# A split-precision decoder trunk on one core: the order of the wide and the narrow products at the end of a column tile

## The chip, the cores and the metric

The kernel runs on one core of a Trainium2 chip. The metric is the device time of one execution in microseconds (us); less is better. Three executions were timed for the kernel before, and one more was taken with the hardware profiler, which is where every row below comes from.

## What is computed

Two layers, each with a SwiGLU feed-forward block, a mixing block and a second SwiGLU block; after each of them a residual is added and a LayerNorm applied. There are 256 tokens of 1024 channels, the feed-forward width is 2816, everything is float32. The change lies in the first two products of the feed-forward block:

```python
def swiglu(x, w_gate, w_up, w_down):
    return (jax.nn.silu(x @ w_gate) * (x @ w_up)) @ w_down

for l in range(DEPTH):
    f = swiglu(x, ffn_w_gate[l, 0], ffn_w_up[l, 0], ffn_w_down[l, 0])
    x = layer_norm(ALPHA * x + 0.5 * f, ln_g[l, 0], ln_b[l, 0])
    z = x @ w_in[l]
    y = ...  # three mixers on column groups of z
    x = layer_norm(ALPHA * x + y @ w_out[l], ln_g[l, 1], ln_b[l, 1])
    f = swiglu(x, ffn_w_gate[l, 1], ffn_w_up[l, 1], ffn_w_down[l, 1])
    x = layer_norm(ALPHA * x + 0.5 * f, ln_g[l, 2], ln_b[l, 2])
```

## The kernel before

**Split operands.** Each float32 operand is held as two float32r halves, a high one and a low one (`split`: ScalarE copies the high half, VectorE subtracts it from the source to get the low half). A product of two split operands is high x high + high x low + low x high, summed in PSUM. The weights `wh` and `wl` are such halves of blocks of 128 x 1024 that arrive by DMA in `raw`; `xT` holds both halves of the transposed activations.

**Column tiles.** Gate and up columns are taken 128 at a time ("T" units; 44 tiles of this kind in the first feed-forward block, 38 in each of the other three). One tile uses one weight block, one of 12 in a ring, and one PSUM bank of 8. The inner dimension of 1024 is walked in eight steps k = 0 to 7 (`KD` is 8). In a step the weights are the stationary operand and the tokens are the moving one:

- the **wide** product, `wh` times `xTb[k]`: 512 columns, since `xTb` shows the high and the low half of the 256 tokens side by side. It fills the whole bank: high x high in the first 256 columns, high x low in the last 256.
- the **narrow** product, `wl` times `xT[k, 0]`: 256 columns, added to the first half of the bank.

`sub_T` calls the step eight times for one tile; then `total` adds the two halves of the bank: ScalarE copies `b[S:]` to `hh`, VectorE adds `b[:S]`. Four tiles (two gate, two up) make a unit, with a Tanh, a multiply and a `split` of the result into `hTh`, `hTl` behind them. In the first feed-forward block `first_unit` computes the first four tiles together instead: there the inner loop goes over four banks, and the outer one over k. The first columns of the other three blocks are done in another form (tokens stationary), and the down projection too; both use products of 512 columns throughout. The mixer's column tiles use `mm_T`, three products of 256 columns in a step.

**Order.** TensorE runs in the order of the program. For ScalarE, VectorE and the DMA queue a list scheduler (`Program.issue`) sets the order from costs and due times; its cost of a product is (columns + 16)/2.4 ns. It writes the order when the program is built; the chip then follows it.

In the step, before the change, the wide product stands first for k = 0 to 6 and last for k = 7. So a tile runs wide, narrow, ... wide, narrow, narrow, wide, and the next tile begins with a wide one.

Of the kernel before, what the change touches and what calls it, by code (L numbers as in the profile page):

```python
# [18 lines left out]
S = 256  # L19
L = 2  # L20
DFF = 2816
KD = D // P
# [256 lines left out]
def build(tc, a):  # L279
# [7 lines left out]
    def ap(v, dtype=None):  # L287
        return v.ap(dtype) if isinstance(v, View) else v
# [35 lines left out]
    def walk(x):  # L324
        return x.rearrange("p (a b c) -> p b a c", b=RUNS, c=RUN)

    def mm(out, lhsT, rhs, start, stop, cost=None, runs=None, both=False):

        cost = cost or (out.n + 16) / 2.4

        def go():
            o, x = ap(out), ap(rhs)
            if runs is not None:
                x = walk(x)[:, runs]
                o = walk(o) if both else o
            T.matmul(out=o, lhsT=ap(lhsT), rhs=x, start=start, stop=stop)  # L336
        pr.add("T", cost, [lhsT, rhs], [out], go)
# [13 lines left out]
    def buf(name, shape, dtype=F32, pool=None, **kw):  # L351
        b = Buf(name, shape, dtype, phase=opened.get(pool), **kw)
        (cbufs if pool is None else phases[pool]).append(b)
        return b
# [21 lines left out]
    xT = buf("xT", (KD, 2, S), F32R, off=OFF_X)  # L376
    xTb = xT.alias((KD, 2 * S))
# [19 lines left out]
    def bank(*shape):  # L397
        b = bank_fifo.pop(0)
        return b.alias(shape) if shape else b
# [27 lines left out]
    ALL = slice(0, RUNS)  # L427
# [12 lines left out]
    def mm_TT(b, h, l, k):  # L440


        def joined(stop):
            mm(b.all, h, xTb[k, :], k == 0, stop, runs=ALL, both=True)

        if k < KD - 1:
            joined(False)
        mm(b[:S], l, xT[k, 0, :], False, False, runs=ALL, both=True)
        if k == KD - 1:
            joined(True)  # L450

    def total(out, b):

# [108 lines left out]
    def ffn(layer, i, ln_prev, nxt, mid=None):  # L562
# [35 lines left out]
        for j, (kind, c0, n) in enumerate(units):  # L598
            if kind == "nat":
                continue  # L600
            f, m = c0 // P, n // P
            if kind == "first":
                first_unit(take(4), th, hh, hTh, hTl)
                continue
            b = take(2 * m)
            for q in range(m):
                pg = bank()
                sub_T(pg, b[q], mm_TT)
                total(hh[q, :], pg)
            act(th[:m, :], hh[:m, :], AF.Tanh, scale=0.5)  # L610
            stt(th[:m, :], th[:m, :], 1.0, hh[:m, :], ALU.add, ALU.mult)
            for _ in range(2):
                if todo:
                    hT(*todo.pop(0))
            for q in range(m):
                pu = bank()
                sub_T(pu, b[m + q], mm_TT)
                total(hh[q, :], pu)
            tt(hh[:m, :], th[:m, :], hh[:m, :], ALU.mult)
            split(hTh[f:f + m, :], hTl[f:f + m, :], hh[:m, :])  # L620
            if mid and j == 3:
                mid()
        return down(hTh, hTl, NF, TAIL, 4.0 * ALPHA, 16.0 * EPS, last, nxt)

    def first_unit(b, th, hh, hTh, hTl):

        accs = [bank() for _ in range(4)]
        for k in range(KD):
            i = b[k // 2] % RING
            for j in range(4):  # L630
                cs = slice((k % 2) * 512 + j * P, (k % 2) * 512 + (j + 1) * P)
                mm_TT(accs[j], wh[i][cs], wl[i][cs], k)
        for j in range(2):
            total(hh[j, :], accs[j])
            act(th[j, :], hh[j, :], AF.Tanh, scale=0.5)
            stt(th[j, :], th[j, :], 1.0, hh[j, :], ALU.add, ALU.mult)
            total(hh[j, :], accs[2 + j])
            tt(hh[j, :], th[j, :], hh[j, :], ALU.mult)
            split(hTh[j, :], hTl[j, :], hh[j, :])
# [224 lines left out]
    b = bank()  # L864
# [127 lines left out]
```

## Time and profile before

| | |
|---|---|
| time, median of 3 (lowest to highest) | 892.92 us (892.76 to 893.49) |
| the profiled execution's own time | 893.46 us |
| its span, first to last instruction | 891.4 us, so 2.06 us lie around it |
| granted TensorE clock, mean | 0.998 of full |
| TensorE (PE), weight loads (PEld) | busy 882.3 us (99%), 781.0 us (88%) |
| VectorE (DVE), ScalarE (ACT) | busy 654.7 us (73%), 483.9 us (54%) |
| DMA queue of the weights | 57.3% of 16 engines' time |

A row of the trace gives the time at which a product starts, and a modelled duration that reaches beyond the start of the next product, since products are pipelined. What a product costs is therefore read from start to start.

### The profile page before, as it was taken

The numbers are of one execution on the slowest core, as the hardware profiler recorded it, in microseconds if no ns is written. First come the engines' busy times: TensorE is split into PE (matmuls) and PEld (weight loads), VectorE is DVE, ScalarE is ACT, GpSimd is POOL, SyncE is SP. The second block draws the span as 40 slices with busy tenths as digits, with TensorE's granted clock in tenths as the row PEclk, the third lists the DMA queues.
The fourth block names the chain that finished last, engine by engine and source line by source line (L and its number), as shares of the span: only waits on it lengthen the run. The fifth ranks groups of instructions, "written<-read, shape, count | busy, mean of one in ns | idle before, by whom it ended". The sixth has DMA issues, their size and how long they took to land.

```text
span 891.4 us, 13272 instructions
## 1 busy us (share of the span) xinstructions
PE 882.3 (99%) x5068; PEld 781.0 (88%) x5068; DVE 654.7 (73%) x971; ACT 483.9 (54%) x707; POOL 22.3 (3%) x33
## 2 busy tenths in 40 slices
PE   9999999999999999999999999999999999999996
PEld 7888888889988888888888888888999888888885
DVE  6999775497898777764697777646979887777515
ACT  6785564267745656644455665543676466555410
POOL 0000000011000000000000000000200000000000
PEclk9999999999999999999999999999999999999999
DMA  8996555467358555555385555553853575555401
GB/s 311 375 314 228 190 192 205 171 221 252 118 187 277 198 189 189 191 206 194 131 281 202 190 195 193 201 190 125 320 208 112 195 271 190 194 201 195 142 1 47
DMA packets 51903, 178.11 MB, mean 200 GB/s; under 512 B 6144, under 2 KB 7936, under 8 KB 51840
## 3 DMA queue, kind: packets, MB, share of 16 engines
q1 hardware_dynamic: 51840, 177.28, 57.3%
q8 instruction: 39, 0.64, 0.3%
q14 instruction: 24, 0.20, 0.1%
HBM read 176.20 MB, written 1.05 MB: 199 GB/s over the span
## 4 chain that ended last, share of the span: by engine, by line
PE 97%; DMA 1%; DVE 1%; SPq 0%; ACT 0%; issue 0%; DVEq 0%
PE bank L336 96%; PE bank L340 1%; DMA raw<-w 1%; DMA x0t<-xT 1%; SPq L346 0%; DVE xn L314 0%; DVE wl L302 0%; ACT wh L296 0%; DVE st L488 0%; DVEq L988 0%; DVE mv L493 0%; DVE ve L309 0%
## 5 line engine op out<-in xcount | busy, mean ns | idle before, releaser
L302 DVE TENSOR_TENSOR wl<-raw,wh 128x1024 fp32r<-128x1024 f32 (+1 forms) x320 | 385.5, 1209 | 155.2 <-ACT wh L296 154.0
L336 PE MATMUL bank<-xT,wh 128*128 128x512 f32 (+1 forms) x1648 | 492.8, 363 | 0.2 <-DVE xT L302 0.2
L296 ACT ACTIVATE wh<-raw 128x1024 fp32r<-128x1024 f32 (+1 forms) x320 | 333.8, 1048 | 235.2 <-PE bank L336 218.4
L336 PE MATMUL bank<-xT,wl 128*128 128x256 f32 x1456 | 377.8, 277 | 0.4 <-DVE wl L302 0.4
L336 PEld LDWEIGHTS bank<-xT,wh 128*128 128x128 f32 x1648 | 285.4, 188 | 38.8 <-DVE xT L302 0.9
L336 PEld LDWEIGHTS bank<-xT,wl 128*128 128x128 f32 x1456 | 273.7, 188 | 12.5 <-DVE wl L302 1.3
L336 PE MATMUL bank<-wl,hTh 128*128 128x512 f32 (+1 forms) x374 | 138.2, 369 | 0.0
L336 PE MATMUL bank<-wh,hTh 128*128 128x512 f32 (+1 forms) x374 | 137.9, 369 | 0.0
L336 PE MATMUL bank<-wh,hTl 128*128 128x512 f32 (+1 forms) x374 | 137.9, 369 | 0.0
L296 ACT ACTIVATE hh<-bank 128x256 f32<-128x256 f32 x158 | 56.5, 374 | 78.2 <-PE bank L336 73.5
L302 DVE TENSOR_TENSOR hh<-bank,hh 128x256 f32<-128x256 f32 x158 | 64.2, 419 | 26.7 <-ACT hh L296 26.6
L336 PEld LDWEIGHTS bank<-wl,hTh 128*128 128x128 f32 x374 | 70.2, 188 | 10.8
L336 PEld LDWEIGHTS bank<-wh,hTh 128*128 128x128 f32 x374 | 70.3, 188 | 10.7
L336 PEld LDWEIGHTS bank<-wh,hTl 128*128 128x128 f32 x374 | 70.2, 188 | 10.6
L336 PE MATMUL bank<-wh,xT 128*128 128x512 f32 (+1 forms) x320 | 79.3, 334 | 0.0
L336 PEld LDWEIGHTS bank<-wh,xT 128*128 128x128 f32 x320 | 54.9, 188 | 6.5 <-DVE xT L302 0.6
L336 PE MATMUL bank<-wl,xT 128*128 128x512 f32 (+1 forms) x160 | 53.0, 331 | 0.0
L314 DVE SCALAR_TENSOR_TENSOR xn<-xn,bank 128x512 f32<-128x512 f32 (+1 forms) x25 | 16.2, 663 | 38.2 <-PE bank L336 38.2
L302 POOL TENSOR_TENSOR rs<-ve,mhalf 128x1 f32<-128x1 f32 x16 | 13.8, 863 | 863.5 <-DVE ve L309 863.5
L336 PEld LDWEIGHTS bank<-wl,xT 128*128 128x128 f32 x160 | 30.1, 188 | 3.1
L296 ACT ACTIVATE hTh<-hh 128x512 fp32r<-128x512 f32 (+1 forms) x42 | 25.4, 605 | 8.4 <-DVE hh L302 8.2
L302 DVE TENSOR_TENSOR hh<-th,hh 128x512 f32<-128x512 f32 (+1 forms) x42 | 27.7, 660 | 1.2
(93 smaller groups left out, 470.3 us busy)
## 6 DMA issues: line engine op xcount, KB each, us to landing
raw<-w SPq DMA_DIRECT2D x312, 512.0 KB, 4.1
gB<-ln_g SPq DMA_DIRECT2D x6, 512.0 KB, 6.5
bB<-ln_b SPq DMA_DIRECT2D x6, 512.0 KB, 6.4
raw<-w SPq DMA_DIRECT2D x8, 256.0 KB, 5.1
x0t<-xT SPq DMA_DIRECT2D x8, 128.0 KB, 4.6
xn<-x SPq DMA_DIRECT2D x2, 512.0 KB, 6.1
out<-xn SPq DMA_DIRECT2D x3, 256.0 KB, 2.0
wT<-sgu_wT SPq DMA_DIRECT2D x2, 256.0 KB, 6.8
```

The lines of the kernel that those rows point to most:

```text
L296: pr.add("A", cost, views(in_, scale, bias), [out], lambda: A.activation(out=ap(out), in_=ap(in_), func=func, scale=ap(scale), bias=ap(bias)))
L302: pr.add(eng, cost, [in0, in1], [out], lambda: e.tensor_tensor(out=ap(out), in0=ap(in0), in1=ap(in1, F32 if as32 else None), op=op))
L314: pr.add("V", cost, views(in0, s, in1), [out], lambda: V.scalar_tensor_tensor(out=ap(out), in0=ap(in0), scalar=ap(s), in1=ap(in1), op0=op0 ...
L336: T.matmul(out=o, lhsT=ap(lhsT), rhs=x, start=start, stop=stop)
L340: pr.add("T", 109.0, [in_, ident.all], [out], lambda: T.transpose(out=ap(out), in_=ap(in_), identity=ap(ident.all)))
```

## The change

The branch that moved the wide product behind the narrow one at k = 7 is gone: in every step the wide product stands first. The bank is closed by the narrow product.

```diff
     def mm_TT(b, h, l, k):
 
 
-        def joined(stop):
-            mm(b.all, h, xTb[k, :], k == 0, stop, runs=ALL, both=True)
-
-        if k < KD - 1:
-            joined(False)
-        mm(b[:S], l, xT[k, 0, :], False, False, runs=ALL, both=True)
-        if k == KD - 1:
-            joined(True)
+        mm(b.all, h, xTb[k, :], k == 0, False, runs=ALL, both=True)
+        mm(b[:S], l, xT[k, 0, :], False, k == KD - 1, runs=ALL, both=True)
```

TensorE, the end of one column tile and the start of the next, in the first feed-forward block. `128x4x32x4` is a wide moving operand, `128x4x16x4` a narrow one; bank_104 is the bank of the tile that ends, bank_105 that of the next.

```order
 L336 MATMUL bank_104<-xT,wl_91 128x4x16x4
 L336 MATMUL bank_104<-xT,wh_79 128x4x32x4
-L336 MATMUL bank_104<-xT,wl_91 128x4x16x4 x2
+L336 MATMUL bank_104<-xT,wl_91 128x4x16x4
 L336 MATMUL bank_104<-xT,wh_79 128x4x32x4
+L336 MATMUL bank_104<-xT,wl_91 128x4x16x4
 L336 MATMUL bank_105<-xT,wh_80 128x4x32x4
 L336 MATMUL bank_105<-xT,wl_92 128x4x16x4
```

Before, two narrow products stood together and then two wide ones, the second of them the next tile's first. Now the two kinds alternate across the end of the tile. The same piece stands at the end of each of the 154 tiles that `sub_T` makes with this step, and in `first_unit` the pair of each of the four banks is turned round at k = 7.

ScalarE, in the second feed-forward block, from its second unit on. `wh` from `raw` is the split of a weight block for a later tile (the ring holds 12), `hh` from a bank is the copy of `total`, `hTh` is the result's high half.

```order
 L296 ACTIVATE wh_79<-raw_72 128x1024
 L296 ACTIVATE hTh<-hh 128x256
-L296 ACTIVATE hh<-bank_100 128x256
-L296 ACTIVATE hh<-bank_104 128x256
+L296 ACTIVATE wh_80<-raw_73 128x1024
+L296 ACTIVATE hh<-bank_104 128x256
+L296 ACTIVATE hh<-bank_100 128x256
 L296 ACTIVATE hTh<-bank_99 128x2x128
 L296 ACTIVATE hTh<-bank_103 128x128
```

The scheduler now puts the split of one more weight block ahead of the two copies that empty the banks, and the same shift by one split goes on to the end of the block's tiles and comes back in the third and the fourth block; VectorE's order follows it. No instruction is added or taken away on any engine, and the DMA queue's order is the same.

## Rows read from the trace of the kernel before

**Rows 1.** The page: the span, and busy time of each engine.

```profile
span 891.4 us, 13272 instructions
...
PE 882.3 (99%) x5068; PEld 781.0 (88%) x5068; DVE 654.7 (73%) x971; ACT 483.9 (54%) x707; POOL 22.3 (3%) x33
```

**Rows 2.** The waits: all that PE waited for, then ScalarE's longest.

```profile
PE bank L336 <- DVE zero L863: 1.3, 1, 1.3
PE bank L336 <- DVE wl L302: 0.4, 2, 0.2
PE bank L336 <- DVE xT L302: 0.2, 1, 0.2
...
ACT wh L296 <- PE bank L336: 218.4, 192, 8.2
```

**Rows 3.** Stretches of column tiles: bounds, length, PE busy (products), clock, DMA.

```profile
20.84:127.36 106.52, 106.52 (x625) 1.00 0.76 266
281.33:295.59 14.26, 14.26 (x88) 1.00 0.78 271
295.61:385.74 90.13, 90.13 (x529) 1.00 0.56 193
```

**Rows 4.** PE in order of time, two column tiles: start, duration, product.

```profile
56.15 0.60 PE L336 MATMUL bank<-xT,wh 128*128 128x512 f32 x2
56.59 0.28 PE L336 MATMUL bank<-xT,wl 128*128 128x256 f32 x1
56.70 0.38 PE L336 MATMUL bank<-xT,wh 128*128 128x512 f32 x1
...
58.59 0.39 PE L336 MATMUL bank<-xT,wl 128*128 128x256 f32 x2
58.82 0.63 PE L336 MATMUL bank<-xT,wh 128*128 128x512 f32 x2
59.29 0.28 PE L336 MATMUL bank<-xT,wl 128*128 128x256 f32 x1
...
61.38 0.39 PE L336 MATMUL bank<-xT,wl 128*128 128x256 f32 x2
61.61 0.60 PE L336 MATMUL bank<-xT,wh 128*128 128x512 f32 x2
62.05 0.28 PE L336 MATMUL bank<-xT,wl 128*128 128x256 f32 x1
```

**Rows 5.** PE in order of time, a tile behind three transposes, and later swaps.

```profile
284.06 0.49 PE L340 MATMUL bank<-ident,hn 128*128 128x128 f32 x3
...
284.62 0.28 PE L336 MATMUL bank<-xT,wl 128*128 128x256 f32 x1
...
285.29 0.28 PE L336 MATMUL bank<-xT,wl 128*128 128x256 f32 x1
...
285.98 0.28 PE L336 MATMUL bank<-xT,wl 128*128 128x256 f32 x1
...
286.65 0.39 PE L336 MATMUL bank<-xT,wl 128*128 128x256 f32 x2
286.88 0.64 PE L336 MATMUL bank<-xT,wh 128*128 128x512 f32 x2
...
289.67 0.60 PE L336 MATMUL bank<-xT,wh 128*128 128x512 f32 x2
```

**Rows 6.** Stretches: inside `first_unit`; then two of mixer tiles, columns as above.

```profile
12.13:15.94 3.81, 3.81 (x24) 1.00 0.99 365
235.59:237.30 1.71, 1.71 (x17) 1.00 0.37 113
236.74:238.45 1.71, 1.71 (x17) 1.00 0.78 287
```

**Rows 7.** The page: ScalarE's split of a weight block, busy us and mean ns.

```profile
L296 ACT ACTIVATE wh<-raw 128x1024 fp32r<-128x1024 f32 (+1 forms) x320 | 333.8, 1048 | 235.2 <-PE bank L336 218.4
```

## The prediction

> **What bounds the kernel.** I read the page first: TensorE is busy 882.3 of 891.4 us [rows 1]. That share counts modelled tails, so the list of waits comes next: TensorE waits 1.3 + 0.4 + 0.2 us in all, never for a free bank and never for ScalarE, while ScalarE waits 218.4 us for TensorE to give a weight buffer of the ring back [rows 2]. The other engines run ahead. The time is the sum of TensorE's steps from start to start, at a granted clock of 1.00, the 2.4 GHz level, in each stretch [rows 3], so an edit counts only as far as it changes these steps.
>
> The stretches of column tiles come third. The first holds 39 tiles (39 x 16 products, plus one whose tail reaches in): 106.52 us, 2.731 us a tile. The last row holds 33 tiles in 90.13 us, again 2.731; the third and fourth feed-forward block have the same row, 90.13 us each [rows 3].
>
> Then the order of time inside two tiles [rows 4]. A reader should take the starts, not the durations. From the narrow product at 56.59 to that at 58.59 lie six wide-narrow pairs: 2.00 us, 0.333 a pair (the wide 0.22, the narrow 0.11: 56.70 less 56.59). Then stand two narrow products (58.59) and two wide ones (58.82, the second opening the next tile). From 59.29 to 61.38 lie six pairs again, of the same sizes: 2.09 us, 0.348 a pair. Then the next swap, at 61.61. From swap to swap the first of these tiles takes 2.67 us (56.15 to 58.82) and the second 2.79 (58.82 to 61.61); the mean is the 2.73 of rows 3. This alternation of a fast and a slow tile repeats through all the long stretches. The columns are the same in both, so the slow tile loses 0.12 us to the order alone: the two wide products after a fast tile take 0.47 (58.82 to 59.29) where those after a slow one take 0.44 (61.61 to 62.05), and the six pairs that follow lose 0.09. A swap that ends a fast tile throws the stream out of its fast pace; a swap that ends a slow one happens to set it right again.
>
> What the stream does when it is thrown out otherwise is seen behind three transposes [rows 5]: from 284.62 two pairs to 285.29 take 0.67, the next two to 285.98 take 0.69, the last two to 286.65 take 0.67. It finds the fast pace inside the tile and keeps it, until the swap (286.88) starts a slow tile that ends at 289.67, 2.79 later. So strict alternation has the fast pace as a resting state, and I see no tile in which it leaves that pace before a swap.
>
> **The change, part by part.**
>
> *Products.* None is added or removed, and none changes its size: 0 us by count.
>
> *The long stretches.* Without swaps the alternation goes on from tile to tile. If it stays at 0.333 a pair, a tile takes 8 x 0.3333 = 2.667 us. First block: 106.52 less 39 x 2.667 (104.01) = 2.51 us. The other three: 90.13 less 33 x 2.667 (88.01) = 2.12 each, 6.36 together. Sum 8.87 us.
>
> *The first five tiles of the three later blocks* take 14.26 us (the row of the second block; the others are within 0.1 of it), with two groups of transposes between [rows 3]. The transposes stay, and the stream has to find its pace behind each. What goes is one slow tile (2.79 instead of 2.667, 0.12 us) and a little behind the fast ones: I take 0.15 a block, 0.45 in all. Bounds: 0, and 14.26 less 5 x 2.667 = 0.92 a block if even the transposes cost nothing.
>
> *`first_unit`.* Four pairs are turned round just ahead of a wait for VectorE's low half, which ends when VectorE is done. I take 0, bounds plus and minus one wide step, 0.22 us.
>
> *The first product of a tile and its wait.* It needs a free bank and a split weight, and was queued behind a wide product; now it stands behind a narrow one, so whatever a satisfied wait costs has 0.11 us of cover instead of 0.22. The nearest row is the mixer's: 256-column products alone, 17 counted in 1.71 us across the end of a tile, and 17 in 1.71 us inside a tile [rows 6]. So I take 0. If the cover were gone it could cost up to a narrow step, 0.11 us a tile; that would undo the gain (below).
>
> *ScalarE and VectorE.* Their order shifts by one split: a bank may be emptied later by that split's 1.05 us [rows 7]. The cover is the ring and the eight banks: a bank is written again eight tiles (some 21 us) later, and TensorE waits for no bank now. I take 0. Were the cover gone, each unit of four tiles would wait those 1.05 us, some 37 us over 35 units: it would show at once. With TensorE faster by 2.3% in these stretches, what would be late next is DMA, at 0.76 of its time in the first block [rows 3]: some 0.78 then, still not full.
>
> *Sum.* 8.87 + 0.45 = 9.3 us. The profiled execution's own time is 893.46 (891.4 and 2.06 around it): 884.1. The median of the runs is 0.54 below that one: 883.6 us, 1.04% less.
>
> **A rule that says otherwise.** The trace shows two paces for the same products at the same clock [rows 4], so neighbours in the order do matter. The Trainium skill ("TensorE: Matmul & The Clock Gate", Step-by-step, on loading the stationary operand) has two independent read ports, and loading the next weights does not steal read bandwidth from the running product. By that a swap would move no time at all, which is the third rival below; the trace of before does not agree for the slow tiles (0.348 a pair against 0.333).
>
> **The rivals.**
>
> 1. *Thrown out once a tile, and back.* The end of a tile (new bank, new weight block, `xT` from k = 0 again, a wait) could disturb the pace as transposes do. The price is that of the transposes: 2.03 us for six pairs against 2.00, 0.03 a tile [rows 5]. A tile takes 2.70; the gain is 0.031 x 138 = 4.3 plus 0.2, so 892.92 less 4.5 = 888.4. For: in the trace every crossing of these tiles has a swap, so an undisturbed one was never seen. Against: the mixer's tiles cross without a trace [rows 6].
>
> 2. *The slow pace is a resting state too.* In `first_unit` wide and narrow products alternate without a swap, and 22 products (24 counted, two of them by their tails) take 3.81 us: 0.346 a pair, held for 11 pairs [rows 6]. If the tiles rest there, each takes 8 x 0.346 = 2.771, 0.040 more than the mean now: 138 x 0.040 = 5.5 us, so 898.4, slower by 0.6%. It decides from 2.731 / 8 = 0.341 a pair on, or from a crossing that costs 0.064 us. For: the same two products in the same order. Against: there the bank changes with every pair and four pairs share one `xTb[k]`; and behind transposes the tiles were seen to leave the slower pairs (0.69 for two) for the faster.
>
> 3. *The order is not the cause.* The slow tiles come from something else that alternates from tile to tile (a bank, a weight buffer, what the other engines do meanwhile) and stay as they are: 892.9. For: slow and fast tiles take turns, as with anything that has a period of two tiles. Against: the loss begins in the two wide products of the swap (0.47 against 0.44) [rows 4], and behind transposes the pace changes inside one tile, in one bank and one weight buffer [rows 5].
>
> **How the numbers follow.** The chance of my forecast (the fast pace held across tiles) is 0.64, of rival 1 0.16, of rival 2 0.11, of rival 3 0.09. The time is the forecast's, 883.6. The low end takes half of the largest gain of the early tiles: 1.4 us instead of 0.45, so 882.6; I go to 882.5. The high end takes in rival 1 with half as much again lost at each crossing (0.045 a tile: 2.712, a gain of 2.6): 890.3, so 890.5. That leaves out rivals 2 and 3, 0.20. The forecast's own range is 882.5 to 885. Faster by over 0.2% (1.8 us, about what a measurement of this kernel can tell from no change): 0.64 + 0.16 = 0.80; within 0.2%: 0.09; slower: 0.11.
>
> **What would show it.** In the trace after, no row of two narrow products in the tiles; the stretches that held 33 tiles last 88.0 us where 90.13 stood, the first block's 39 tiles 104.0; pairs step by 0.333 across the ends of tiles, and the first wide of a tile follows the narrow before it by 0.11. TensorE's waits stay under 2 us. Rival 1 would show a few steps over 0.34 at each tile's start, rival 2 0.346 throughout. The forecast fails if the first wide product starts late, if the pace at a block's start settles at 0.346, or if TensorE waits for a bank.

## The result, and the profile after

The changed kernel takes 883.92 us, the median of 3 runs (883.39 to 884.58), against 892.92. The ratio is 0.9898, 95% interval 0.9876 to 0.9921: 9.0 us, 1.0% faster. The forecast was 883.6. The profiled execution after is the fastest of its three, 883.39 us with a span of 881.3; its clock is 0.998 as before.

The page and the waits of the kernel after, beside [rows 1, 2]:

```profile
span 881.3 us, 13264 instructions
...
PE 872.4 (99%) x5068; PEld 779.8 (88%) x5068; DVE 651.5 (74%) x971; ACT 484.3 (55%) x707; POOL 22.3 (3%) x33
```

```profile
PE bank L336 <- DVE zero L857: 1.3, 1, 1.3
PE bank L336 <- DVE wl L302: 0.3, 1, 0.3
PE bank L336 <- DVE xT L302: 0.2, 1, 0.2
...
ACT wh L296 <- PE bank L336: 281.7, 234, 8.2
```

TensorE has as many products as before and is busy 9.9 us less; it still waits for no bank and hardly for weights. ScalarE waits longer for TensorE than before (281.7 against 218.4 us), though TensorE is faster: its order now puts the splits earlier, so it meets a full ring more often. The wait goes with that order: in the first two experiments below it is 204.5 us with the old order of ScalarE and 292.3 with the new one.

Stretches of column tiles after (bounds, length, PE busy, clock, DMA), beside [rows 3]: the first block's 39 tiles, then the second block's first five and its other 33.

```profile
20.26:124.24 103.98, 103.98 (x626) 1.00 0.77 272
278.16:292.30 14.14, 14.14 (x88) 1.00 0.80 291
292.32:380.30 87.98, 87.98 (x530) 1.00 0.57 198
```

The same 39 tiles took 106.52 us and take 103.98; the 33 took 90.13 and take 87.98 (the other two blocks have 87.98 too); the first five fell from 14.26 to 14.14. In order of time there are no pairs of like products left; this is TensorE across the end of a tile, beside [rows 4]:

```profile
35.80 0.28 PE L336 MATMUL bank<-xT,wl 128*128 128x256 f32 x1
35.91 0.38 PE L336 MATMUL bank<-xT,wh 128*128 128x512 f32 x1
36.13 0.28 PE L336 MATMUL bank<-xT,wl 128*128 128x256 f32 x1
36.25 0.38 PE L336 MATMUL bank<-xT,wh 128*128 128x512 f32 x1
36.47 0.28 PE L336 MATMUL bank<-xT,wl 128*128 128x256 f32 x1
```

The narrow product at 36.13 closes a tile and the wide one at 36.25 opens the next, 0.12 later; the narrow starts at 35.80, 36.13 and 36.47 are 0.33 apart on both sides. The crossing leaves no mark.

### The profile page after: what moved, and what is told of

It reads as the page before. It is cut to its first block, busy times and chain, and to the rows that moved or that the text cites. A ratio compares the mean times of both kernels' runs of the same rounds, so it can differ in the third digit from the quotient of the medians.

```text
span 881.3 us, 13264 instructions
## 1 busy us (share of the span) xinstructions
PE 872.4 (99%) x5068; PEld 779.8 (88%) x5068; DVE 651.5 (74%) x971; ACT 484.3 (55%) x707; POOL 22.3 (3%) x33
## 4 chain that ended last, share of the span: by engine, by line
PE 97%; DMA 1%; DVE 1%; SPq 0%; ACT 0%; issue 0%; DVEq 0%
PE bank L336 96%; PE bank L340 1%; DMA raw<-w 1%; DMA x0t<-xT 1%; SPq L346 0%; DVE xn L314 0%; DVE wl L302 0%; ACT wh L296 0%; DVE st L482 0%; DVEq L982 0%; DVE mv L487 0%; DVE ve L309 0%
## 5 line engine op out<-in xcount | busy, mean ns | idle before, releaser
L296 ACT ACTIVATE wh<-raw 128x1024 fp32r<-128x1024 f32 (+1 forms) x320 | 333.6, 1048 | 298.9 <-PE bank L336 281.7
L336 PE MATMUL bank<-xT,wl 128*128 128x256 f32 x1456 | 401.8, 276 | 0.3 <-DVE wl L302 0.3
L336 PEld LDWEIGHTS bank<-xT,wh 128*128 128x128 f32 x1648 | 296.3, 188 | 42.2 <-DVE xT L302 0.9
L302 DVE TENSOR_TENSOR hh<-bank,hh 128x256 f32<-128x256 f32 x158 | 59.8, 417 | 0.0
L296 ACT ACTIVATE hh<-bank 128x256 f32<-128x256 f32 x158 | 51.3, 373 | 5.9 <-DVE hTl L302 2.4
L302 DVE TENSOR_TENSOR hTl<-hh,hTh 128x512 fp32r<-128x512 f32 (+1 forms) x42 | 27.5, 654 | 0.0
```

The costliest lines, as they stand in the source:

```text
L296: pr.add("A", cost, views(in_, scale, bias), [out], lambda: A.activation(out=ap(out), in_=ap(in_), func=func, scale=ap(scale), bias=ap(bias)))
L302: pr.add(eng, cost, [in0, in1], [out], lambda: e.tensor_tensor(out=ap(out), in0=ap(in0), in1=ap(in1, F32 if as32 else None), op=op))
```

## The experiments

The name *pace* stands for the step from one wide-narrow pair to the next. Each kernel is compared with the kernel before on the same chip; the interval is 95%.

**Order of TensorE or order of the others?** The change moves two products a tile, and with that the scheduler reorders ScalarE and VectorE. Two kernels take these apart: they give the scheduler one order and issue the other.

```diff
+        wide, narrow = (b.all, h, xTb[k, :]), (b[:S], l, xT[k, 0, :])
+        end = k == KD - 1
+        one, two = (narrow, wide) if end else (wide, narrow)
+        mm(*one, k == 0, False, runs=ALL, both=True, emit=wide)
+        mm(*two, False, end, runs=ALL, both=True, emit=narrow)
```

This is the first; in the second the places of (`wide`, `narrow`) and (`one`, `two`) are exchanged. `emit` names the operands that the product is issued with.

> TensorE's products in the order of the change (wide and narrow alternate throughout), ScalarE's and VectorE's order as before the change: the scheduler still plans the swap, and the two products are exchanged when they are issued. Theory (the order of the products alone sets the pace): each tile 2.667 us, time 883.9 us, within 1 us of the change. Rival (the gain comes from the order of the other engines, which split one weight block earlier): 892.9 us, slow and fast tiles in turn as before.

> The mirror: products swapped at k = 7 as before the change, ScalarE's and VectorE's order as after it. Theory: 892.9 us, tiles of 2.68 and 2.78 us in turn. Rival (the other engines' order): 883.9 us.

The first took 884.37 us, ratio 0.9898 (0.9883 to 0.9913); the second 893.57, ratio 0.9998 (0.9989 to 1.0008). Tiles of the first block: 39 of the first kernel, then 38 of the second, which take 2.73 us each as before the change:

```profile
18.95:122.93 103.98, 103.98 (x626) 1.00 0.80 276
```

```profile
21.44:125.16 103.72, 103.72 (x609) 1.00 0.77 268
```

With the old order on ScalarE and VectorE the first kernel's tiles take what they take after the change, to 0.01 us. The whole gain is in the order of TensorE's products, and the reordering of the other engines is worth nothing.

**The end of the tile, or the swap?** The swap is kept, but stands at k = 3.

```diff
+        one, two = (narrow, wide) if k == 3 else (wide, narrow)
+        mm(*one, k == 0, False, runs=ALL, both=True)
+        mm(*two, False, k == KD - 1, runs=ALL, both=True)
```

> The swap stands in the middle of each tile (k = 3) instead of at its end; the tile is closed by the narrow product and the next one opened by the wide one, as after the change. Theory (any swap throws the stream out or sets it right, wherever it stands): 892.9 us within 1.5, slow and fast stretches of eight pairs in turn, from k = 4 to the next k = 3. Rival (it is the end of a tile that matters: bank, wait, signal of the last product): 883.9 us.

It took 893.65 us, ratio 1.0003 (0.9993 to 1.0012). TensorE in order of time:

```profile
30.22 0.39 PE L336 MATMUL bank<-xT,wl 128*128 128x256 f32 x2
30.45 0.63 PE L336 MATMUL bank<-xT,wh 128*128 128x512 f32 x2
30.92 0.28 PE L336 MATMUL bank<-xT,wl 128*128 128x256 f32 x1
...
33.01 0.39 PE L336 MATMUL bank<-xT,wl 128*128 128x256 f32 x2
33.24 0.60 PE L336 MATMUL bank<-xT,wh 128*128 128x512 f32 x2
33.68 0.28 PE L336 MATMUL bank<-xT,wl 128*128 128x256 f32 x1
```

These are the intervals of [rows 4]: the wide pair 0.47 (30.45 to 30.92), then six pairs in 2.09 (30.92 to 33.01), then a swap whose wide pair takes 0.44. The slow stretch now runs across the end of a tile. What happens at a tile's end (new bank, wait, closing product) has no part in it.

**Does each swap cost, or only every second one?** Half the swaps are taken away, every other one.

```diff
+        one, two = (narrow, wide) if swap and k == KD - 1 else (wide, narrow)
...
-                sub_T(pg, b[q], mm_TT)
+                sub_T(pg, b[q], mm_TT if q else mm_sw)
```

> The swap at k = 7 in every other tile only (the first of each pair of gate or up tiles), 80 swaps instead of 154. Theory (a swap out of the fast pace throws the stream out, and only the next swap, or some nine pairs of alternation, brings it back): there is no second swap to set it right, so each swap costs its whole way back, about 0.16 us (seven pairs of the slow tile, then two more, read from the trace before): 883.9 + 77 x 0.16 = 896.2 us, slower than with twice as many swaps. Rival (each swap has a price of its own, 9.0 us over 154 of them): 883.9 + 80 x 0.058 = 888.6 us.

It took 895.45 us, ratio 1.0027 (1.0018 to 1.0036): slower than the kernel with all the swaps. From one swap to the next, two tiles on:

```profile
42.30 0.64 PE L336 MATMUL bank<-xT,wh 128*128 128x512 f32 x2
42.78 0.28 PE L336 MATMUL bank<-xT,wl 128*128 128x256 f32 x1
...
45.21 0.28 PE L336 MATMUL bank<-xT,wl 128*128 128x256 f32 x1
45.33 0.40 PE L336 MATMUL bank<-xT,wh 128*128 128x512 f32 x1
45.56 0.28 PE L336 MATMUL bank<-xT,wl 128*128 128x256 f32 x1
45.68 0.38 PE L336 MATMUL bank<-xT,wh 128*128 128x512 f32 x1
...
47.57 0.39 PE L336 MATMUL bank<-xT,wl 128*128 128x256 f32 x2
47.80 0.63 PE L336 MATMUL bank<-xT,wh 128*128 128x512 f32 x2
```

Two tiles take 5.50 us (42.30 to 47.80) where 2 x 2.667 is 5.33. After the swap eight pairs pass at 0.35 (42.78 to 45.56: 2.78); from 45.56 on, the pace is 0.333 again (six pairs to 47.57 in 2.01). So a single swap costs 0.16 us: 0.11 of it in these eight pairs of the way back, 0.04 in its two wide products (0.48 from 42.30 to 42.78, where two steps of 0.22 make 0.44). In the kernel before, the next swap cut that way short after one tile.

**Which half of the swap?** The two narrow neighbours and the two wide ones are set apart: every second tile is turned round (narrow, wide) from k = 1 on.

```diff
+        one, two = (narrow, wide) if turned and k > 0 else (wide, narrow)
...
-                sub_T(pg, b[q], mm_TT)
+                sub_T(pg, b[q], mm_turned if q else mm_TT)
```

> The two halves of the swap stand apart: in every second tile the products from k = 1 on are turned round (narrow, then wide), so two narrow products meet after that tile's first pair, and two wide ones seven pairs later, at its end. Theory A (the two narrow products throw the stream out, since the product behind them starts late): the turned tile is slow from its first pairs on. Theory B (the two wide products throw it out): the turned tile keeps 0.333 a pair and the tile behind it is slow. If neither alone does it: 2.667 us a tile and 884 us. With A or B some 0.1 us per pair of tiles is lost: 890 to 896 us.

It took 891.33 us, ratio 0.9976 (0.9965 to 0.9987). The tile from 29.52 to 32.26 stands behind two wide neighbours; the one from 32.26 is turned and has two narrow ones at its start and two wide ones at its end.

```profile
29.30 0.60 PE L336 MATMUL bank<-xT,wh 128*128 128x512 f32 x2
29.74 0.28 PE L336 MATMUL bank<-xT,wl 128*128 128x256 f32 x1
...
32.15 0.28 PE L336 MATMUL bank<-xT,wl 128*128 128x256 f32 x1
32.26 0.38 PE L336 MATMUL bank<-xT,wh 128*128 128x512 f32 x1
32.48 0.39 PE L336 MATMUL bank<-xT,wl 128*128 128x256 f32 x2
...
32.94 0.28 PE L336 MATMUL bank<-xT,wl 128*128 128x256 f32 x1
...
34.66 0.28 PE L336 MATMUL bank<-xT,wl 128*128 128x256 f32 x1
34.78 0.60 PE L336 MATMUL bank<-xT,wh 128*128 128x512 f32 x2
...
35.22 0.28 PE L336 MATMUL bank<-xT,wl 128*128 128x256 f32 x1
...
37.22 0.28 PE L336 MATMUL bank<-xT,wl 128*128 128x256 f32 x1
...
37.88 0.39 PE L336 MATMUL bank<-xT,wl 128*128 128x256 f32 x2
...
38.33 0.28 PE L336 MATMUL bank<-xT,wl 128*128 128x256 f32 x1
...
40.03 0.28 PE L336 MATMUL bank<-xT,wl 128*128 128x256 f32 x1
```

Behind the two wide products at 29.30 seven pairs take 2.41 (29.74 to 32.15), 0.344 each, so two wide neighbours throw the stream out without narrow ones beside them (theory B); the fast pace had been back for only a few pairs when they came. Behind the two narrow ones at 32.48, where the pace had just been found again (32.15 to 32.48), five pairs take 1.72 (32.94 to 34.66), 0.344 each too (theory A). And the two wide ones at 34.78 set it right: from 35.22 six pairs take 2.00. The narrow ones at 37.88 come after an even fast stretch (eight pairs in 2.66 from 35.22) and cost something there too, though less: five pairs take 1.70 (38.33 to 40.03) where 5 x 0.333 is 1.67. Neither theory alone holds: either half throws the stream out, and the two wide ones set it right when they meet it slow; that two narrow ones can do so is not shown.

**What are the two paces made of?** Next, the reads. The same two kernels with the moving operand read, and the bank written, in plain order instead of interleaved runs of 4.

```diff
-        mm(b.all, h, xTb[k, :], k == 0, False, runs=ALL, both=True)
-        mm(b[:S], l, xT[k, 0, :], False, k == KD - 1, runs=ALL, both=True)
+        mm(b.all, h, xTb[k, :], k == 0, False)
+        mm(b[:S], l, xT[k, 0, :], False, k == KD - 1)
```

> The change, with the moving operand and the output of these products read and written in plain order instead of in interleaved runs of 4; nothing else. In the fast pace a wide product steps 220 ns and a narrow one 113, where 512 and 256 columns at 2.4 GHz are 213.3 and 106.7. If the 6.7 ns come from the interleaved order, plain reads are faster: up to 154 x 16 x 6.7 ns = 16 us less, 867 us at best. If the interleaved order is what makes the fast pace possible (no clash of the product's reads with the next weight load), each pair gets longer: at the 0.348 us of the slow tiles 884 + 154 x 0.12 = 902 us.

> The kernel before, swap at k = 7, with the same plain reads. If the two paces come of the interleaved reads meeting the weight loads, they are gone here or have another size, and the swap costs nothing: the same time as the change with plain reads within 1 us. If the swap costs by itself, whatever the reads are, it is some 9 us slower than that one.

The change with plain reads took 907.97 us, ratio 1.0164 (1.0147 to 1.0181); the kernel before with plain reads 905.99, ratio 1.0142 (1.0127 to 1.0157). Tiles, 38 in the first block and 28 in the second, of the change with plain reads, then of the kernel before with them:

```profile
21.02:127.40 106.38, 106.38 (x610) 1.00 0.76 260
301.76:380.88 79.12, 79.12 (x450) 1.00 0.56 186
```

```profile
20.55:127.41 106.86, 106.86 (x609) 1.00 0.75 262
301.79:380.55 78.76, 78.76 (x449) 1.00 0.57 188
```

The tiles of the change take 2.80 in the first block and 2.83 in the second (0.350 and 0.353 a pair, somewhat over the 0.348 of the expectation), those with the swap 2.81 in both. So the interleaved order is needed for 2.667 where the weights lie now, and dropping it does not win back the 6.7 ns. Reads and bank writes went to plain order together; which of them counts is not shown. With plain order the swap costs nothing overall: the kernel with it is 2.0 us faster, which neither theory said. In the rows above it loses 0.48 us in the first block's tiles and gains 0.36 in the second's, and much of the 2.0 us is not traced to these tiles.

**Where the weights lie.** The order on all engines is that of the change; the weight buffers start at another place within a line of 64 elements (`OFF_W`; the moving operand starts at 4).

```diff
-OFF_W = 16
+OFF_W = 32
```

> The change, with all weight buffers 16 elements (64 bytes) further on in SBUF (16 becomes 32 within a line of 64), and nothing else: the order on all engines is the same. If the pace depends on where the next weights lie against the moving operand (reads that clash), the step of a pair changes, up to the 0.348 us of the slow tiles, 902 us; it can't fall below 0.333 unless the 6.7 ns above are a clash too. If only the order counts: 883.9 us.

> The change with the weight buffers 8 elements further on (24 instead of 16 in a line of 64). If the pace depends on where the weights lie against the moving operand, a value between or beyond: 884 to 902 us, and a pair between 0.333 and 0.348. If only the shift by whole 64 bytes mattered: as at 16 (884) or as at 32 (902).

> The change with the weight buffers 8 elements back (8 instead of 16), which is nearer to the moving operand's own 4. Same theories: a place nearer to the moving operand's lines should clash otherwise than 16; the step of a pair says how much. A pair below 0.333 would show that the 6.7 ns a product above the columns are a clash too.

At 32 the time is 901.91 us, ratio 1.0096 (1.0081 to 1.0112); at 24 it is 925.85, ratio 1.0362 (1.0343 to 1.0381); at 8 it is 904.66, ratio 1.0125 (1.0107 to 1.0144). Stretches of whole tiles; at 32 these are 38 of the first block:

```profile
19.80:124.48 104.68, 104.68 (x610) 1.00 0.77 266
```

at 24 these are 34 of the first block:

```profile
29.44:127.34 97.90, 97.90 (x546) 1.00 0.71 249
```

and at 8 these are 37 of the first block and 29 of the second:

```profile
20.83:121.45 100.62, 100.62 (x594) 1.00 0.78 271
300.09:380.49 80.40, 80.40 (x466) 1.00 0.57 190
```

A tile takes 2.755 us with the weights at 32, 2.88 at 24, and at 8 it takes 2.72 in one block and 2.77 in the other; at 16 it takes 2.667. The theory that only the order counts fell here: with no edit to the order, the place of the weights changes the pace. At 24 and at 8 the times lie above the 902 us that I had allowed, and at 24 the pair, 0.360, above the 0.348. At 8 one order holds two paces in one execution, 0.340 a pair over 37 tiles and 0.347 over 29. No place that was tried gave less than 0.333 a pair.

**The change once more, and the mixer in the same form.** The mixer's 24 column tiles use three 256-column products a step. The second kernel gives them the wide-narrow form, with `total` behind each.

```diff
         def col():
             b = bank()
-            sub_T(b[:S], take(1)[0])
-            return b
+            sub_T(b, take(1)[0], mm_TT)
+            c = cs.pop(0)
+            cs.append(c)
+            total(c.all, b)
+            return c
```

> The change itself once more, beside the next kernel on one chip: 884 us, ratio to before 0.990. In its profile every tile at 2.667 us again; the first unit may show another pace than in the profile of the change, since it starts when the first transfers happen to land.

> The change, and the mixer's 24 column tiles computed in the wide-narrow form too (two products in a step instead of three, the halves of the bank added by ScalarE and VectorE as in the feed-forward tiles). Three narrow products took 0.344 us a step there, a pair at the fast pace takes 0.333: 24 x 8 x 0.011 = 2.1 us less, less some 0.03 to 0.16 us for each of the four or five places per layer where other products stand between the tiles and the stream must find its pace again: 882 to 884 us. Rival (the added copies and sums make the last tiles late, and the output projection waits for them): over 884 us, with a wait of TensorE for yTh or yTl.

The change took 883.6 us again, ratio 0.9899 (0.9882 to 0.9916), and its 39 tiles take the same 103.98 us:

```profile
20.42:124.40 103.98, 103.98 (x626) 1.00 0.79 273
```

The mixer in the wide-narrow form took 892.78, ratio 0.9995 (0.9986 to 1.0004), so it gives the whole gain away. Its waits, and the stretch of the first mixer:

```profile
PE bank L336 <- DVE xr L314: 6.9, 6, 1.5
```

```profile
206.00:250.00 44.00, 40.56 (x227) 1.00 0.36 124
```

TensorE is idle for 3.44 of these 44 us; in the kernel after it is not idle from 204 to 246, its own mixer stretch. The rival held in its time and its kind, though not in its place: the sums and copies come late, and TensorE waits for `xr`, where I had named `yTh` or `yTl`. These waits are 6.9 of the 9.2 us that were lost; the rest is not traced. The pace was not what I expected either, in the last three tiles of this mixer, behind transposes:

```profile
234.49 0.28 PE L336 MATMUL bank<-xT,wl 128*128 128x256 f32 x1
...
242.46 0.28 PE L336 MATMUL bank<-xT,wl 128*128 128x256 f32 x1
```

From 234.49 to 242.46 lie 23 pairs, 0.3465 each: the slow resting pace of [rows 6], in column tiles, without a swap.

## Why the prediction was right

*What bounds the kernel.* TensorE's starts were the right thing to add up: its waits stayed under 2 us, and the first experiment shows that the new order of the other engines is worth nothing.

*The long stretches.* 2.51 us forecast for the first block, 2.54 measured (106.52 less 103.98); 2.12 for each of the others, 2.15 measured. *The first five tiles*: 0.15 forecast for a block, 0.12 measured in the second (14.26 less 14.14). *The crossing* of a tile's end: 0 forecast, none seen.

*`first_unit`* was put at 0, within 0.22 us, and this term was mis-sized: the stretch of 39 tiles begins at 20.26 instead of 20.84, so 0.58 us came from ahead of it, and not from the four turned pairs. One part is the pace: the order is the same up to k = 7, but 32 products (two more counted by their tails) go at 0.333 a pair in the kernel after, where [rows 6] had 0.346, some 0.2 us over these 16 pairs.

```profile
11.67:16.99 5.32, 5.32 (x34) 1.00 1.01 399
```

A larger part is a wait of TensorE for VectorE's low half in the kernel before, where a narrow product starts 0.73 behind its wide one; after, the steps there are the usual 0.22:

```profile
10.15 0.49 PE L336 MATMUL bank<-xT,wh 128*128 128x512 f32 x1
10.88 0.38 PE L336 MATMUL bank<-xT,wl 128*128 128x256 f32 x1 [0.23 <-DVE wl L302]
```

Smaller differences of either sign make up the rest. The start moves by more than that between kernels with the same order on TensorE: the 39 tiles begin at 20.26 in the kernel after, at 20.42 in its repeat and at 18.95 in the first experiment. So I call this half microsecond luck of the start. The same alternation does rest at 0.333 in one execution and at 0.346 in another. The two profiles in which the first unit ends with the swap (before, and the second experiment) show 0.346, six without a swap there 0.333; the swap comes only behind these pairs, so why they differ is open. With the 0.58, the long stretches (2.54 and 3 x 2.15) and the early tiles (0.12, 0.20 and 0.12) make 10.0 of the 10.1 us by which the spans differ. Without it they make 9.4, near the 9.3 forecast and the 9.0 by which the medians differ; the profiled execution before was among the slower ones and the one after the fastest of its three.

*Rival 1* (thrown out at each crossing) fell in the profile after. *Rival 3* (the order is not the cause) fell with the first three experiments. By the Trainium skill ("TensorE: Matmul & The Clock Gate", Step-by-step) loading the next weights takes no read bandwidth from the running product. By that alone the place of the weights would not matter, and in the runs with shifted weights it does: with the order unchanged, 16 elements further on cost 0.09 us a tile, 8 elements further on 0.21. The measurement decides that the place counts; it does not show that the load is what takes the time.

*Rival 2* (the slow pace is a resting state too) did not come about in the tiles, but its mechanism is real, more than I gave it: the mixer experiment held it for 23 pairs, and with the weights at 8 the same order held either of two paces for tens of tiles. In the change each entry into the tiles (the stall ahead of the first block's tiles, the start of a block, the transposes) led to the fast pace. I had seen transposes do so in the trace, not explained it, and it stays unexplained why the transposes of that mixer lead to the other. That the change stayed clear of rival 2 was in this part luck.

*What stays open.* That the load of the next weights and the reads of the moving operand get in each other's way is what the shifts point to, and the plain order too as far as it is the reads; no row of the trace shows such a clash itself, so it is argued, not shown. Nor is it known why the fast pace has 6.7 ns a product above its columns.

## What to carry to other kernels

Where TensorE is the bound and never waits, read its steps from start to start: equal products at two paces, at the same clock, are time that a mere reordering may give back, as it did here. Look for the regular pattern that lasts, keep it unbroken across the ends of tiles, and count a break with its way back (0.16 us here), not at its own instructions alone. Try the order, the interleaving of the operand and the place of the weights within a line together: each was worth 1 to 5% here, and the better order changed when the interleaving went; the place was tried with one order and one interleaving only.

## What the runs showed of the hardware

- One order of products can rest at two paces at a granted clock of 1.00 (the 2.4 GHz level): 0.333 us a pair through whole blocks and 0.3465 for 23 pairs of the mixer experiment; with the weights at 8, 0.340 over 37 tiles and 0.347 over 29. What decides between them is not shown.
- The place of the weight buffers within a line of 64 elements changes the step of a pair with no other edit: 0.340 to 0.347 at 8, 0.333 at 16, 0.360 at 24, 0.344 at 32.
- Fewer disturbances can be slower: on one chip 80 swaps took 895.45 us, 154 swaps 893.4, and none (the first experiment's kernel) 884.37.
